# First mixer of a two-layer backbone: gate products on quarters of the array, ScalarE in order of issue, another order of the parts

## The chip, the cores and the metric

The kernel runs on one core of a Trainium2 chip. The metric is the device time of one execution in microseconds (us); lower is better. TensorE is called PE in the rows, VectorE DVE, ScalarE ACT, GpSimd POOL, and the queue of SyncE that issues nearly all DMAs is SP.

## What is computed

The reference is a backbone of two layers. Each layer has a SwiGLU sub-layer of half weight, a token mixer, and a second SwiGLU; each sub-layer is wrapped in RMSNorm with shift, scale and gate. There are 256 latent and 256 context tokens of width 1024. In the first layer the mixer runs on all 512 tokens. Its input projection has seven column groups: the RG-LRU's input and gate (512 columns each), three of 256 for a short gated convolution, and two of 256 for chunked spatial gating. The RG-LRU is what the change is about:

```python
def lru_coeffs(xc, w_r, b_r, w_i, b_i, lam):      # xc: tokens x 512, 8 heads of 64
    xh = xf.reshape(B, L, LRU_HEADS, HEAD_DIM)
    r = sigmoid(einsum('blhi,hij->blhj', xh, w_r) + b_r)
    i = sigmoid(einsum('blhi,hij->blhj', xh, w_i) + b_i)
    log_a = -LRU_C * r * softplus(-lam)
    a = exp(log_a)
    bx = sqrt(-expm1(2.0 * log_a)) * (i * xf)
    return a, bx                                  # for each of two directions
...
h = linear_scan(a, b, h0)                         # h[t] = a[t] h[t-1] + b[t]
o_lru = gelu(lru_gate) * (h_forward + h_backward)
```

The three branches are concatenated to 1024 channels and go through one output projection.

## The kernel before

**Layout.** Channels lie on the 128 partitions and the 512 tokens along the free axis. A matrix product of a weight tile is three products in a rounded type (`hi` x `hh`, `hi` x `hl`, `lo` x `hh`), so one unit of 128 output channels is 8 x 3 = 24 products of 512 columns. The raw weights come by DMA (`raw`, 512 KB), ScalarE casts them to `hi` in two halves, and VectorE subtracts for `lo` in two halves (`split`, L169). The gates' products are plain fp32.

**Parts of the mixer.** The mixer is written as parts with one letter each: `c`, `x`, `b` are the three units of the short convolution's channel groups 0 and 1 (`short_c`, `short_x`, `short_b`, L756 to L784), `g` the RG-LRU's gate branch (`gate`, L691), `v`, `u`, `m` the spatial gating (`chunk_v`, `chunk_u`, `chunk_mix`, L788 to L819). The RG-LRU's four channel groups (128 channels, two heads each) go through `C` (`lru_conv`, L709: one ScalarE and three VectorE instructions), `G` (`lru_gates`, L712: four products against `wbd`, four sigmoids, two multiplications), `D` (`lru_decay`, L726: for each direction an exponential, a tanh and three VectorE instructions) and `S` (`lru_scan`, L738: square roots, scans, the sum of the two directions, the gate, and `put`). `put` (L684) splits a finished group into `oh` (a cast on ScalarE) and `ol` (a subtraction on VectorE), the moving operands of the output projection.

**The gates' weights.** `wbd` of a channel group is one DMA of 256 KB: for each direction and gate a 128 x 128 matrix with the two heads' 64 x 64 blocks on its diagonal and zeros elsewhere. A group is four products of 128 x 128 by 512 columns (L717, L721), each with a PSUM bank of its own; `pbank` (L103) has six banks, and a product into a bank waits until the bank's last reader is done.

**What sets the order.** In the mixer PE runs in the order of the string `ORDER[0]` (`manual_schedule` with PE alone); the other engines' orders come from the scheduler. `unit` (L675) keeps three weight units in the queue. ScalarE holds one table of functions at a time; a sigmoid, an exponential or tanh, a square root and a GELU each need another, and a change is an `ACT_TABLE_LOAD`; copies, casts and scaled copies go with any.

**The output projection** (`out_phase`, L319) takes the channels in the order 4, 5, 6, 7, 0, 1, 2, 3, that is `b0`, `b1`, `m0`, `m1` and then the four RG-LRU groups. After it come the norms of the sub-layer and the second SwiGLU.

Of the kernel before, what the change touches and what calls it, by code (L numbers as in the profile page):

```python
# [8 lines left out]
F32 = mybir.dt.float32  # L9
# [36 lines left out]

LATE = ((0,), (1, 2, 3))
MANUAL = {mybir.EngineType.PE}

ORDER = ("c1 C0 g3 G0 C1 C2 C3 D0 c0 x1 G1 G3 D3 x0 S0 D1 v0 S3 G2 b0 g2 D2 u0 m0 S1 b1 u1 m1 S2",  # L50
         "c0 x0 C1 C0 C3 C2 g3 g2 G1 G0 D1 D0 c1 b0 u0 v0 S1 w0 G3 u1 x1 b1 m1 w1 S0 m0 G2 w2 p1 w3 w4 w5 p2 p5 w6 D2 S2 w7 p0 "
         "D3 S3 p7 p4 p3 p6")

TAIL = 4

# [26 lines left out]
def backbone(ctx: ExitStack, tc: tile.TileContext, xT, vecs, crow, w_mod, w_in, w_out, w_mi, w_mo, w_lru, w_cm, b_cm, lam, w_last, out):  # L82
# [20 lines left out]
    def pbank():  # L103
        return ps.tile([P, 512], F32, tag="mm", name=nm("mm"))
# [525 lines left out]
    def mixer(l, segs, nxt, plan, skew_out, order_of, next_unit=None):  # L630
# [77 lines left out]

        def lru_conv(c):  # L709
            xcs[c] = conv(c)  # L710

        def lru_gates(c):  # L712
            wbd = tp.tile([P, 4, P], F32, tag="wbd", name=nm("wbd"))
            nc.sync.dma_start(wbd, w_lru[l, c])
            for c, d, b in heads[2 * c:2 * c + 2]:
                pr = pbank()
                pe.matmul(pr, lhsT=wbd[:, 2 * d, :], rhs=xcs[c], start=True, stop=True)  # L717
                r = rs[c, d] = tt_()
                sc.activation(r, pr, AF.Sigmoid, bias=V("b_r", b))
                pi = pbank()  # L720
                pe.matmul(pi, lhsT=wbd[:, 2 * d + 1, :], rhs=xcs[c], start=True, stop=True)  # L721
                i = ix[c, d] = tt_()
                sc.activation(i, pi, AF.Sigmoid, bias=V("b_i", b))
                ve.tensor_tensor(i, i, xcs[c], op=OP.mult)

        def lru_decay(c):  # L726
            for c, d, b in heads[2 * c:2 * c + 2]:
# [114 lines left out]
        def out_part(k):  # L842
            for m in range(KT):
                out_mm(m, (k,))

        parts = dict(w=out_load, p=lambda m: out_mm(m, (4, 5, 6, 7)), g=gate, c=short_c, x=short_x, b=short_b, v=lambda _: chunk_v(), u=chunk_u, m=chunk_mix,
                     C=lru_conv, G=lru_gates, D=lru_decay, S=lru_scan)
        def issue():
            for part in order_of.split():
                parts[part[0]](int(part[1]))  # L850

        if len(segs) == 2:
            with tc.manual_schedule(engines=MANUAL):
# [5 lines left out]
            def load(m):
                hi, lo = unit()  # L860
                return (lambda k: hi[:, order[k], :]), (lambda k: lo[:, order[k], :])

            out_phase(range(KT), load, [oh[k] for k in order], [ol[k] for k in order], y, KT,
                      ranges(segs, skew_out), norms.on_y, 0, 1)
            return


# [383 lines left out]
```

## Time and profile before

| | us |
|---|---|
| median of 3 runs | 1642.15 (1640.8 to 1643.95) |
| the profiled execution: its own time | 1642.21 |
| the profiled execution: its span | 1640.4 |
| PE busy | 1612.5 |
| DVE busy | 1164.3 |
| ACT busy | 736.7 |
| POOL busy | 120.3 |

A span is the stretch from the first to the last instruction that the profile shows. Times such as 452.80 are us from its start. A row of a timeline gives the start, the duration, and the engine, line and operation, with the count of instructions that were merged; neighbouring instructions of one engine overlap by their tails, so what an instruction costs its engine is the step from its start to the next start. A matmul in fp32 shows as two records. The first mixer lies between about 441 and 572 us; its parts run on PE from 441.6 to 524.8, its output projection after that.

### The profile page before, as it was taken

How to read it: one execution, taken by the hardware profiler on the slowest of the kernel's cores; microseconds unless marked ns; L12 is line 12 of the kernel's file. 1: busy time of each engine (PE TensorE's matmuls, PEld its weight loads, DVE VectorE, ACT ScalarE, POOL GpSimd, SP SyncE). 2: the span in 40 equal slices, each digit the busy share in tenths (PEclk: the TensorE clock that was granted, in tenths of full speed). 3: DMA queues.
4: the chain of work that ended last, by engine and by line, in shares of the span. 5: the costliest groups of instructions: out<-in, count | busy, mean ns of one | idle time of the engine just before them, and what ended most of it. 6: DMA issues, size and time to landing. Idle time of an engine off the chain costs nothing.

```text
span 1640.4 us, 23432 instructions
## 1 busy us (share of the span) xinstructions
PE 1612.5 (98%) x8846; PEld 1371.6 (84%) x8846; DVE 1164.3 (71%) x2183; ACT 736.7 (45%) x1378; POOL 120.3 (7%) x166
## 2 busy tenths in 40 slices
PE   6999999999999999999999999999999999999998
PEld 3788888889977998888888998888888998789997
DVE  4899898548788787867763887767432788785554
ACT  5523322244697662332233462332232479864543
POOL 0000000005000500000000410000000410100000
PEclk9999999999999999999999999999999999999999
DMA  9577677431323225655552215655422316155552
GB/s 370 189 218 261 205 229 223 144 121 44 103 72 120 77 97 187 221 162 174 179 164 80 100 61 194 222 166 167 141 90 90 103 54 210 47 167 194 180 191 78
DMA packets 73906, 249.97 MB, mean 152 GB/s; under 512 B 8384, under 2 KB 10048, under 8 KB 73792
## 3 DMA queue, kind: packets, MB, share of 16 engines
q1 hardware_dynamic: 73216, 247.94, 45.9%
q8 instruction: 69, 1.13, 0.3%
q10 hardware_dynamic: 576, 0.52, 0.1%
q14 instruction: 45, 0.37, 0.1%
HBM read 247.39 MB, written 1.05 MB: 151 GB/s over the span
## 4 chain that ended last, share of the span: by engine, by line
PE 89%; DVE 6%; ACT 3%; DMA 1%; issue 1%; POOL 0%; SPq 0%; POOLq 0%; DVEq 0%; ACTq 0%
PE mm L113 87%; PE st L113 1%; DVE x L271 1%; DVE sq L394 1%; DVE t L703 0%; PE mod L113 0%; DVE z L270 0%; DVE tmp L262 0%; DMA x<-in_xT 0%; ACT hi L173 0%; DVE t L397 0%; POOL rs L241 0%; DVE t L332 0%; DMA raw<-in_w_mi 0%; ACT t L730 0%
## 5 line engine op out<-in xcount | busy, mean ns | idle before, releaser
L173 ACT CAST hi<-raw 128x512 fp32r<-128x512 f32 (+1 forms) x596 | 343.6, 610 | 672.7 <-PE mm L113 475.8
L113 PE MATMUL mm<-hh,hi 128*128 128x512 f32 (+1 forms) x1840 | 625.6, 348 | 0.5 <-ACT hh L1095 0.2
L113 PE MATMUL mm<-hl,hi 128*128 128x512 f32 (+1 forms) x1840 | 622.5, 346 | 1.8 <-DVE hl L256 1.0
L174 DVE TENSOR_TENSOR lo<-raw,hi 128x512 fp32r<-128x512 f32 (+1 forms) x596 | 387.5, 680 | 157.3 <-ACT hi L173 154.5
L113 PE MATMUL mm<-hh,lo 128*128 128x512 f32 (+1 forms) x1840 | 466.6, 346 | 0.0
L113 PEld LDWEIGHTS mm<-hh,hi 128*128 128x128 f32 x1840 | 345.5, 188 | 52.1 <-ACT hh L1095 2.8
L113 PEld LDWEIGHTS mm<-hl,hi 128*128 128x128 f32 x1840 | 345.9, 188 | 51.2 <-DVE hl L1101 1.6
L113 PEld LDWEIGHTS mm<-hh,lo 128*128 128x128 f32 x1840 | 325.1, 188 | 47.2
L196 DVE SCALAR_TENSOR_TENSOR junk<-raw,cb 128x1024 bf16<-128x1024 f32 x256 | 312.9, 1222 | 70.8 <-DMA raw<-in_w_mod 67.1
L113 PE MATMUL mm<-t,hi 128*128 128x512 f32 (+1 forms) x1056 | 240.6, 367 | 0.0
L113 PEld LDWEIGHTS mm<-t,hi 128*128 128x128 f32 x1056 | 182.8, 188 | 35.7 <-issue 0.2
L397 POOL TENSOR_TENSOR t<-t,sq 128x256 f32<-128x256 f32 x112 | 94.2, 856 | 712.2 <-ACT sq L391 702.3
L113 PE MATMUL mm<-t,lo 128*128 128x512 f32 (+1 forms) x528 | 131.5, 367 | 0.0
L113 PEld LDWEIGHTS mm<-t,lo 128*128 128x128 f32 x528 | 92.6, 188 | 17.7
L480 DVE TENSOR_TENSOR sg<-sg,mm 128x512 f32<-128x512 f32 (+1 forms) x72 | 45.9, 640 | 78.3 <-PE mm L113 78.3
L113 PE MATMUL mm<-t,hh 128*128 128x256 f32 x512 | 71.2, 281 | 0.0
L113 PEld LDWEIGHTS mm<-t,hh 128*128 128x128 f32 x512 | 65.7, 188 | 0.5
L173 ACT CAST t<-sg 128x512 fp32r<-128x512 f32 (+1 forms) x94 | 50.6, 541 | 32.0 <-DVE sg L480 29.0
L332 DVE TENSOR_TENSOR t<-t,mm 128x256 f32<-128x256 f32 (+1 forms) x66 | 35.4, 536 | 29.3 <-PE mm L113 29.1
L174 DVE TENSOR_TENSOR t<-sg,t 128x512 fp32r<-128x512 f32 (+1 forms) x94 | 55.3, 589 | 0.9 <-ACT t L173 0.9
L113 PE MATMUL mm<-hi,t 128*128 128x512 f32 x176 | 55.1, 394 | 0.0
L263 ACT ACTIVATE hh<-tmp,modv 128x256 fp32r<-128x256 f32 x72 | 42.4, 596 | 22.1 <-DVE tmp L262 21.9
(179 smaller groups left out, 1212.4 us busy)
## 6 DMA issues: line engine op xcount, KB each, us to landing
raw<-in_w_in SPq DMA_DIRECT2D x176, 512.0 KB, 3.6
raw<-in_w_mod SPq DMA_DIRECT2D x128, 512.0 KB, 4.3
raw<-in_w_out SPq DMA_DIRECT2D x48, 512.0 KB, 3.3
raw<-in_w_mi SPq DMA_DIRECT2D x36, 512.0 KB, 4.1
raw<-in_w_last SPq DMA_DIRECT2D x22, 512.0 KB, 3.3
raw<-in_w_out SPq DMA_DIRECT2D x24, 384.0 KB, 3.7
t<-in_w_mod SPq DMA_DIRECT2D x32, 256.0 KB, 5.8
raw<-in_w_mo SPq DMA_DIRECT2D x8, 512.0 KB, 3.7
```

The costliest lines, as they stand in the source:

```text
L113: te.matmul(dst, lhsT=lhsT, rhs=rhs, start=start, stop=stop)
L173: sc.copy(hi, src)
L174: ve.tensor_tensor(lo, src, hi.bitcast(F32), op=OP.subtract)
L196: ve.scalar_tensor_tensor(junk, raw.rearrange("p k c -> p (k c)"), 1.0, cb[:, s], op0=OP.mult, op1=OP.mult, accum_out=modv[l][:, v, m, s:s ...
L263: sc.activation(hh[:, m, a:b], tmp, AF.Identity, scale=A, bias=B)
L271: ve.scalar_tensor_tensor(x[:, m, a:b], z, mcol(l, 3 * i + 2, m, s), x[:, m, a:b], op0=OP.mult, op1=OP.add)
L332: ve.tensor_tensor(y[m][:, a:b], y[m][:, a:b], p[:, :b - a], op=OP.add)
L394: ve.scalar_tensor_tensor(q[2], y, G, x[:, m, a:b], op0=OP.mult, op1=OP.mult)
L397: (gp if JACC[c] == "g" else ve).tensor_tensor(acc[c], acc[c], q[c], op=OP.add)
L480: ve.tensor_tensor(sg[:, :b - a], sg[:, :b - a], pu[:, :b - a], op=OP.mult)
```

## The change

Four things change, all in the first mixer (`l` = 0, both segments); layer 1's order string is only rewritten for the new letters.

1. **Gates on quarters** (`QUARTERS`). The 64 x 64 blocks alone are multiplied. For each direction and gate there are two products, each on 64 rows of the array and 64 of its columns: gate `r` reads partitions 0 to 63, gate `i` partitions 64 to 127, head 0 writes partitions 0 to 63 of the bank and head 1 partitions 64 to 127. So that both gates find both heads in their rows, a copy of the convolution's result with its halves exchanged (`swap`, two tiles) is made by two DMAs from POOL's queue in `C`. The weights come in four DMAs of 32 KB instead of one of 256 KB. There are 32 products of 64 x 64 instead of 16 of 128 x 128, and 8 POOL DMAs and 12 SP DMAs more.
2. **ScalarE in order of issue.** In the first mixer's parts ScalarE, too, runs in the written order.
3. **Another `ORDER[0]`.** The short convolution's and the gates' parts are placed anew; square roots are a part of their own (`R`) ahead of the scans (`S`), `put` is a part of its own (`H`), and `l4`, `l5` fill the queue of weight units to four or five.
4. **Output projection.** The first five output tiles are begun (`EARLY`) with channels 4 to 7, twelve products each, and ended later with channels 0 to 3.

```diff
-ORDER = ("c1 C0 g3 G0 C1 C2 C3 D0 c0 x1 G1 G3 D3 x0 S0 D1 v0 S3 G2 b0 g2 D2 u0 m0 S1 b1 u1 m1 S2",
+IN_ORDER = {mybir.EngineType.PE, mybir.EngineType.Activation}
+ORDER = ("c1 C0 C1 g3 C2 C3 c0 G0 G1 l4 D0 D1 x1 l5 R0 R1 S0 S1 G3 x0 l5 G2 D3 D2 H0 b0 l5 H1 v0 g2 l4 u0 R3 R2 m0 S3 b1 "
+         "u1 m1 l4 S2 H3 H2",
...
         def lru_conv(c):
             xcs[c] = conv(c)
+            if l in QUARTERS:
+                lru_swap(c)
+        def lru_swap(c):
+            t = turned_xc[c] = tp.tile([P, T], F32, tag="swap", name=nm("swap"), bufs=2)
+            for a, b in ((0, P // 2), (P // 2, 0)):
+                gp.dma_start(t[a:a + P // 2], xcs[c][b:b + P // 2])
+        def gate_products(c):
...
+                        nc.sync.dma_start(wbd[64 * g:64 * g + 64, :, h], src[a:a + 64, :, g, a:a + 64])
...
+            def products(d):
+                ps2 = pbank(), pbank()
+                for g, p in enumerate(ps2):
...
+                    for h in range(2):
+                        src = (xcs if g == h else turned_xc)[c]
+                        rows, cols = slice(64 * g, 64 * g + 64), slice(64 * h, 64 * h + 64)
+                        pe.matmul(p[cols], lhsT=wbd[rows, d, h], rhs=src[rows], start=True, stop=True)
+                return ps2
...
         def lru_gates(c):
-            wbd = tp.tile([P, 4, P], F32, tag="wbd", name=nm("wbd"))
-            nc.sync.dma_start(wbd, w_lru[l, c])
+            products = gate_products(c)
             for c, d, b in heads[2 * c:2 * c + 2]:
-                pr = pbank()
-                pe.matmul(pr, lhsT=wbd[:, 2 * d, :], rhs=xcs[c], start=True, stop=True)
+                pr, pi = products(d)
...
+        def lru_root(c):
+            for d in range(2):
+                sc.activation(rs[c, d], rs[c, d], AF.Sqrt, scale=-1.0)
         def lru_scan(c):
...
-                sc.activation(h, h, AF.Sqrt, scale=-1.0)
...
-            put(c, h)
+        def lru_put(c):
+            put(c, rs[c, 1])
...
-            with tc.manual_schedule(engines=MANUAL):
+            with tc.manual_schedule(engines=IN_ORDER if l in QUARTERS else MANUAL):
                 issue()
...
+            for item in todo[:EARLY]:
+                begun.append(begin(item))
+            for i, (m, a, b) in enumerate(todo):
+                p = begun[i] if i < EARLY else begin(todo[i])
+                half(p, m, a, b, 1)
+                sc.copy(y[m][:, a:b], p[:, :b - a])
+                norms.on_y(m, a, b)
```

How the change moves instructions shows on two engines. In the names the first number is the buffer's. On PE, group 2's gates of the kernel before stand between `v0` (the last products of `mm_667`) and `b0` (`mm_682`):

```order
L113 MATMUL mm_667_4272<-hi_649_4112,hl_80 128x256
L113 MATMUL mm_671_4313<-t_615_3960,wbd_670_4311 128x512
L113 MATMUL mm_673_4317<-t_615_3960,wbd_670_4311 128x512
L113 MATMUL mm_675_4322<-t_615_3960,wbd_670_4311 128x512
L113 MATMUL mm_677_4326<-t_615_3960,wbd_670_4311 128x512
L113 MATMUL mm_682_4339<-hh_79,hi_657_4178 128x512
```

After the change the same gates are eight quarter products, between `x0` (`mm_661`) and `b0` (`mm_680`), with no `v0` ahead of them; `mm_666`, `mm_667`, `mm_670` and `mm_671` are their four banks:

```order
L119 MATMUL mm_661_4185<-hh_79,lo_614_3965 128x512
L119 MATMUL mm_666_4231<-t_608_3946,wbd_665_4226 64x512
L119 MATMUL mm_666_4231<-swap_609_3951,wbd_665_4226 64x512
L119 MATMUL mm_667_4232<-swap_609_3951,wbd_665_4226 64x512
L119 MATMUL mm_667_4232<-t_608_3946,wbd_665_4226 64x512
L119 MATMUL mm_670_4242<-t_608_3946,wbd_665_4226 64x512
L119 MATMUL mm_670_4242<-swap_609_3951,wbd_665_4226 64x512
L119 MATMUL mm_671_4243<-swap_609_3951,wbd_665_4226 64x512
L119 MATMUL mm_671_4243<-t_608_3946,wbd_665_4226 64x512
L119 MATMUL mm_680_4281<-hh_79,hi_636_4053 128x512
```

Group 2's gates now stand ahead of `v0`, right behind `x0`; each bank takes two products, and the last bank used before them is `x0`'s instead of one of `v0`'s. On ScalarE, the sigmoids of groups 1 and 3 in the kernel before (L719 and L723 are the sigmoids, L741 the square root, L730 the exponential):

```order
L719 ACT_TABLE_LOAD
L719 ACTIVATE t_630_4062<-mm_629_4060,vec_76 128x512
L723 ACTIVATE t_632_4066<-mm_631_4064,vec_76 128x512
L719 ACTIVATE t_634_4071<-mm_633_4069,vec_76 128x512
L723 ACTIVATE t_636_4075<-mm_635_4073,vec_76 128x512
L719 ACTIVATE t_639_4082<-mm_638_4080,vec_76 128x512
L723 ACTIVATE t_641_4086<-mm_640_4084,vec_76 128x512
L741 ACT_TABLE_LOAD
L741 ACTIVATE t_611_3948<-t_611_3948 128x512
L719 ACT_TABLE_LOAD
L719 ACTIVATE t_643_4091<-mm_642_4089,vec_76 128x512
L723 ACTIVATE t_645_4095<-mm_644_4093,vec_76 128x512
```

After the change group 3's sigmoids (`mm_653` to `mm_658`) come behind the square roots of groups 0 and 1, and those behind the casts of two weight units and the last tanh (L771 is the tanh, L780 the square root, L761 and L763 the sigmoids):

```order
L771 ACTIVATE t_633_4046<-t_633_4046,s4_100 128x512
L179 CAST hi_647_4126<-raw_646_4124 128x512 x2
L179 CAST hi_650_4134<-raw_649_4132 128x512 x2
L780 ACT_TABLE_LOAD
L780 ACTIVATE t_620_4008<-t_620_4008 128x512
L780 ACTIVATE t_624_4019<-t_624_4019 128x512
L780 ACTIVATE t_629_4035<-t_629_4035 128x512
L780 ACTIVATE t_633_4046<-t_633_4046 128x512
L761 ACT_TABLE_LOAD
L761 ACTIVATE t_655_4169<-mm_653_4163,vec_76 128x512
L763 ACTIVATE t_656_4171<-mm_654_4164,vec_76 128x512
L761 ACTIVATE t_659_4180<-mm_657_4174,vec_76 128x512
```

ScalarE now does one function for several groups before it changes the table, and the sigmoids that free group 3's banks stand further back in its queue.

## Rows read from the trace of the kernel before

**Rows 1.** The page: busy time of PE, and the chain by engine.

```profile
PE 1612.5 (98%) x8846; PEld 1371.6 (84%) x8846; DVE 1164.3 (71%) x2183; ACT 736.7 (45%) x1378; POOL 120.3 (7%) x166
...
PE 89%; DVE 6%; ACT 3%; DMA 1%; issue 1%; POOL 0%; SPq 0%; POOLq 0%; DVEq 0%; ACTq 0%
```

**Rows 2.** Busy time by window: start:end, length, PE PEld DVE ACT POOL, clock.

```profile
480.00:490.00 10.00, 10.00 (x88) 10.00 (x87) 10.00 (x21) 9.92 (x16) 0.00 (x0) 1.00 0.08 29
```

**Rows 3.** All waits of PE between 400 and 600: total, times, longest.

```profile
PE st L113 <- POOL t L397: 0.2, 1, 0.2
```

**Rows 4.** Timeline of PE: a unit of 24 products, and three gate blocks.

```profile
447.20 0.40 PE L113 MATMUL mm<-hh,hi 128*128 128x512 f32 x1
...
452.80 3.59 PE L113 MATMUL mm<-t,wbd 128*128 128x512 f32 x8
...
456.46 0.39 PE L113 MATMUL mm<-hl,hi 128*128 128x512 f32 x1
...
467.43 7.03 PE L113 MATMUL mm<-t,wbd 128*128 128x512 f32 x16
...
474.52 0.39 PE L113 MATMUL mm<-hl,hi 128*128 128x512 f32 x1
```

**Rows 5.** Timeline of PE: fp32 products on 32 columns, and on 64 (`chunk_mix`).

```profile
34.54 1.93 PE L113 MATMUL mod<-t,cs 128*32 128x512 f32 x16
...
36.73 0.40 PE L113 MATMUL mm<-hl,hi 128*128 128x512 f32 x1
...
511.41 1.09 PE L113 MATMUL mm<-wcm,t 128*64 128x128 f32 x16
```

**Rows 6.** Timeline of ACT: casts, table load, sigmoids, exponentials, square roots, GELUs.

```profile
437.03 3.25 ACT L173 CAST hi<-raw 128x512 fp32r<-128x512 f32 x6
...
454.41 1.28 ACT L719 ACT_TABLE_LOAD   x1
455.70 0.69 ACT L719 ACTIVATE t<-mm,vec 128x512 f32<-128x512 f32 x1
...
458.00 2.24 ACT L701 ACTIVATE t<-t,vec 128x512 f32<-128x512 f32 x3
...
461.55 1.34 ACT L730 ACTIVATE t<-t,s 128x512 f32<-128x512 f32 x2
...
484.77 1.16 ACT L741 ACTIVATE t<-t 128x512 f32<-128x512 f32 x2
...
491.12 1.21 ACT L798 ACTIVATE t<-mm 128x256 f32<-128x256 f32 x4
```

**Rows 7.** Timeline of DVE: the decay's instructions, a convolution step, the scans.

```profile
482.01 1.29 DVE L732 SCALAR_TENSOR_TENSOR t<-t,t 128x512 f32<-128x512 f32 x2
...
484.42 0.76 DVE L735 TENSOR_SCALAR t<-t 128x512 f32<-128x512 f32 x2
485.09 0.48 DVE L778 SCALAR_TENSOR_TENSOR t<-zc,vec,t 128x256 f32<-128x256 f32 x1
...
488.48 1.22 DVE L744 TENSOR_TENSOR_SCAN t<-t,t 128x512 f32<-128x512 f32 x1
489.61 0.67 DVE L747 TENSOR_TENSOR_SCAN t<-t,t 128x256 f32<-128x256 f32 x1
```

**Rows 8.** DMA issues of the gates' weights between 425 and 530: size, us to landing.

```profile
wbd<-in_w_lru SPq DMA_DIRECT2D x4, 256.0 KB, 2.9
```

**Rows 9.** Timeline of DVE: one instruction beside busy POOL, and after it.

```profile
540.24 0.96 DVE L394 SCALAR_TENSOR_TENSOR sq<-t,modv,x 128x256 f32<-128x256 f32 x1
...
550.95 0.48 DVE L394 SCALAR_TENSOR_TENSOR sq<-t,modv,x 128x256 f32<-128x256 f32 x1 [0.53 <-ACT t L330]
```

**Rows 10.** Windows in the second mixer's end, columns as in rows 2.

```profile
1434.00:1438.00 4.00, 3.02 (x26) 2.94 (x24) 3.14 (x6) 1.60 (x4) 0.00 (x0) 0.93 0.37 110
1438.00:1442.00 4.00, 4.00 (x20) 3.87 (x19) 2.43 (x11) 1.62 (x3) 1.90 (x2) 0.50 0.43 155
1442.00:1446.00 4.00, 2.69 (x12) 1.99 (x11) 3.32 (x10) 2.29 (x4) 0.39 (x1) 0.72 0.38 133
```

More of the change, by code (lines that the diff above doesn't have):

```diff
@@ L37 @@
 NSQ = 3
+QUARTERS = (0,)
+EARLY = 5
 JACC = 'gvg'
@@ L710, in lru_conv @@
             xcs[c] = conv(c)
+            if l in QUARTERS:
+                lru_swap(c)
+        turned_xc = {}
+        def lru_swap(c):
[3 more added lines that the diff above has]
+        def gate_products(c):
+            if l in QUARTERS:
+                wbd = tp.tile([P, 2, 2, P // 2], F32, tag="wbd", name=nm("wbd"))
+                for g in range(2):
+                    for h in range(2):
+                        a = 64 * h
+                        src = w_lru[l, c].rearrange("p (d g) o -> p d g o", g=2)
+                        nc.sync.dma_start(wbd[64 * g:64 * g + 64, :, h], src[a:a + 64, :, g, a:a + 64])
+            else:
+                wbd = tp.tile([P, 4, P], F32, tag="swap", name=nm("wbd"))
+                nc.sync.dma_start(wbd, w_lru[l, c])
+            def products(d):
+                ps2 = pbank(), pbank()
+                for g, p in enumerate(ps2):
+                    if l not in QUARTERS:
+                        pe.matmul(p, lhsT=wbd[:, 2 * d + g, :], rhs=xcs[c], start=True, stop=True)
+                        continue
+                    for h in range(2):
+                        src = (xcs if g == h else turned_xc)[c]
+                        rows, cols = slice(64 * g, 64 * g + 64), slice(64 * h, 64 * h + 64)
+                        pe.matmul(p[cols], lhsT=wbd[rows, d, h], rhs=src[rows], start=True, stop=True)
+                return ps2
+            return products
         def lru_gates(c):
-            wbd = tp.tile([P, 4, P], F32, tag="wbd", name=nm("wbd"))
-            nc.sync.dma_start(wbd, w_lru[l, c])
+            products = gate_products(c)
             for c, d, b in heads[2 * c:2 * c + 2]:
-                pr = pbank()
-                pe.matmul(pr, lhsT=wbd[:, 2 * d, :], rhs=xcs[c], start=True, stop=True)
+                pr, pi = products(d)
                 r = rs[c, d] = tt_()
                 sc.activation(r, pr, AF.Sigmoid, bias=V("b_r", b))
-                pi = pbank()
-                pe.matmul(pi, lhsT=wbd[:, 2 * d + 1, :], rhs=xcs[c], start=True, stop=True)
                 i = ix[c, d] = tt_()
@@ L736, in lru_decay @@
                 es[c, d] = e
+        def lru_root(c):
+            for d in range(2):
+                sc.activation(rs[c, d], rs[c, d], AF.Sqrt, scale=-1.0)
         def lru_scan(c):
-            for c, d, _ in heads[2 * c:2 * c + 2]:
+            for d in range(2):
                 e, h, b = es[c, d], rs[c, d], ix[c, d]
-                sc.activation(h, h, AF.Sqrt, scale=-1.0)
                 ve.tensor_tensor(b, b, h, op=OP.mult)
@@ L846, in mixer @@
         parts = dict(w=out_load, p=lambda m: out_mm(m, (4, 5, 6, 7)), g=gate, c=short_c, x=short_x, b=short_b, v=lambda _: chunk_v(), u=chunk_u, m=chunk_mix,
-                     C=lru_conv, G=lru_gates, D=lru_decay, S=lru_scan)
+                     C=lru_conv, G=lru_gates, D=lru_decay, R=lru_root, S=lru_scan, H=lru_put, l=fill)
         def issue():
@@ L857, in mixer, with half, begin @@
             y = norms.y = [tt_() for _ in range(KT)]
[L859 to L864, printed above, removed]
+            todo, begun, ws = ranges(segs, skew_out), [], {}
+            def half(p, m, a, b, i):
+                hi, lo = ws[m]
+                ops = [(hi, x_, k) for k in order[4 * i:4 * i + 4] for x_ in (oh, ol)]
+                ops += [(lo, oh, k) for k in order[4 * i:4 * i + 4]]
+                for j, (w, x_, k) in enumerate(ops):
+                    pe.matmul(p[:, :b - a], lhsT=w[:, k, :], rhs=x_[k][:, a:b], start=i == j == 0, stop=i == 1 and j == len(ops) - 1)
+            def begin(item):
+                if item[0] not in ws:
+                    ws[item[0]] = unit()
+                p = pbank()
+                half(p, *item, 0)
+                return p
+            for item in todo[:EARLY]:
[5 more added lines that the diff above has]
+                norms.on_y(m, a, b)
             return
@@ L873, in mixer @@
         need(nxt[0], 3 * nxt[1] + 1)
-        with tc.manual_schedule(engines=MANUAL):
+        with tc.manual_schedule(engines=IN_ORDER if l in QUARTERS else MANUAL):
             issue()
@@ L877, in mixer @@
                 out_part(k)
-        with tc.manual_schedule(engines=MANUAL2):
+        with tc.manual_schedule(engines=MANUAL2 | IN_ORDER if l in QUARTERS else MANUAL2):
             pieces = unit_pieces(next_unit)
```

4 lines of the change are left out of this document (2 added, 2 removed).

## The prediction

> **What bounds the kernel now.** I read the page first, then the windows over the first mixer, then PE's waits, then the timelines. PE is busy in 1612.5 of 1640.4 us and is 89% of the chain that ended last [rows 1]. In the mixer it is busy without a break: the window at 480 shows 10.00 of 10 us at clock 1.00, and between 400 and 600 PE's waits come to 0.2 us [rows 2, 3]. So the mixer now costs what PE's columns cost, and whatever ScalarE or VectorE saves there is worth nothing by itself. But the same window has VectorE at 10.00 and ScalarE at 9.92 [rows 2]: PE is only just ahead of two full engines. The question is whether they still keep pace when PE does its gates earlier and in less time.
>
> **The change part by part.** The sum is made against the profiled execution, 1642.21 us, which is the median within 0.1 us.
>
> Gate products, removed: a unit of 24 products takes 5.60 us (447.20 to 452.80), a product 0.233. The first gate block begins at 452.80; the next unit's second product begins at 456.46, its first 0.23 earlier, so four gate products take 3.43 us, 0.857 each, and the double block 6.86 (467.43 to 474.52, less 0.23) [rows 4]. The third block equals the first: 16 products, 13.7 us.
>
> Gate products, added: 32 quarter products of as many columns. If four run side by side, they cost 8 x 0.857 = 6.9 us, a gain of **6.9**; if two, 13.7 and no gain; if none, 27.4 and a loss of 13.7. No row shows products on half the rows. The nearest are eight fp32 products of 32 columns of the array: from 34.54 to the next product (36.73 less 0.23) they take 1.96 us, which is 0.98 for four against 4 x 0.857 alone, so four ran together, with about 0.1 us at each change of shape [rows 5]. I take four together, and 8 changes at 0.1: +0.8. The Trainium skill, "TensorE: Matmul & The Clock Gate", Part 3 (Packing small matmuls), says that weights are loaded beside running products only where the row group differs; the two heads of a gate here share one. By it only pairs would run together (a rival below); the rows just read, four column tiles in one row group, speak against it.
>
> ScalarE's table: the new order changes tables 9 times less at 1.29 us (454.41 to 455.70) [rows 6]. PE does not wait for ScalarE there now, so that is worth nothing by itself. What counts is where each result stands in ScalarE's queue, which is now fixed.
>
> First new wait, at G2. In the new order `c1 g3 c0` are the units at 441.6, 447.2 and 452.8, so `c0` ends at 458.4. ScalarE's copy of `c0` stands ahead of the sigmoids. By steps [rows 6]: cast or copy 3.25/6 = 0.54, table 1.29, sigmoid (458.00 - 455.70)/4 = 0.575, exponential or tanh 0.62 (1.34 for two, less a tail of 0.1), square root 0.58 (1.16 for two). So: copy to 459.1; table 460.4; eight sigmoids of G0 and G1 465.0; four casts (`l4`) 467.1; table 468.4; eight exponentials and tanh 473.4, and 0.4 for tanh that now follow their own exponential, 473.8; four casts (`l5`) 476.0; table 477.2; four square roots 479.5; table 480.8; three of G3's sigmoids 482.5. PE meanwhile: G0 and G1 458.4 to 462.1, and 0.25 because G1's last banks wait for G0's sigmoids; `x1` to 468.0; G3 to 469.8; `x0` to 475.4; G2 would end at 477.2. But there are six banks: four hold G3's results, one `x0`'s, and G2 has four to write. Its second, third and fourth wait for G3's first three sigmoids, so G2's last pair of products starts at 482.6 and ends at 483.1. New wait: **+5.9** us. `b0` and all behind it on PE stand in the queue.
>
> Second new wait, at `m1`. VectorE works off the decays without a break from the first tanh (about 469.8). I count 64 instructions up to `b0`'s product: 35 at 0.60, 8 at 0.33, 15 short ones at 0.39, 4 half scans at 0.6, 2 scans at 1.13 [rows 7] = 34 us, so it ends about 504. ScalarE comes to the cast of `b0` about 493 and, being in order, stands there until VectorE has made it, 504.7. Behind it: four casts, a table, `v0`'s GELUs (1.21 for four [rows 6]), `g2`'s 0.6, and the cast of `u1`'s weights, to 510.5; VectorE needs that cast, idles from 507, and then has 27 instructions (19 at 0.60, 4 at 0.6, 2 at 1.13, and 1.6 of waits) before `m1`'s last product: 17.7 us, to 528.3, product 528.9, ScalarE's cast 529.5. PE hides most: from 483.2 `b0` 5.6, `v0` 11.2, `g2` 5.6, `u0` 5.6, `m0` 0.9 [rows 5], `b1` 5.6, `u1` 5.6, `m1` 0.9 come to 524.2, and twelve products of the two first output tiles with three of the four channels to 527.0. New wait: about +2.7, and some 0.6 for the third tile's parked weights, whose casts ScalarE has behind it: **+3.3**. Later channels (0 to 3) are covered by the other begun tiles.
>
> At nothing: the swaps (4 pairs of DMAs). C0's and C1's convolutions end near 452 and 452.5 on VectorE, G0 and G1 need them at 458.4 and 460.3; the nearest landing is 2.9 us [rows 8]. C2's and C3's wait for G0's and G1's products, and their users G3 and G2 are ahead of ScalarE anyway. The 12 more SP issues, the earlier weights and layer 1's `wbd` in the swaps' tiles cost SP time while SP has units in hand; if that cover went, one landing, 2.9. Begun output tiles: same products.
>
> Sum: -6.9 + 0.8 + 0.25 + 5.9 + 3.3 = **+3.35**: 1645.6 us. Both waits are set by ScalarE and VectorE, so what PE saves or loses ahead of them moves the sum little.
>
> **The rivals.**
> A, no new wait: ScalarE or VectorE get through 6 to 7 us faster than their rows say, and the quarters' gain shows. For it: PE had no wait at all before with more table loads [rows 3]. Against: 23 us of the chain to G3's sigmoids are counted in rows. -6.9 + 1.0 = 1636.3.
> B, the forecast: 1645.6; own range 1643 to 1648.
> C, pairs only, or the change doesn't do what it says: no gain on PE, but the wait at G2 shrinks from 5.9 to 1.5 since ScalarE sets its end, so only +1.8 more: 1647.4. If none runs together, PE is the bound again: 1642.2 + 13.7 + 0.8 and the second wait, about 1659.
> D, slower by late swaps: POOL issues four DMAs between 452 and 458 while VectorE runs the convolutions. VectorE's L394 takes 0.96 beside busy POOL and 0.48 after it [rows 9]: the two hinder each other. It decides from 4 p + 2.9 = 8.3, p = 1.3 us for one issue on POOL; at p = 2, G1 starts 2.6 late, the whole ScalarE queue moves with it: 1648.2. The Trainium skill, "SBUF — State Buffer" (A bandwidth-pool intuition that's wrong), gives such a DMA about 0.62 us alone and 3.1 beside a copy on VectorE; by 3.1, worked out as an estimate, it would be 7 late and 1652. No row shows a DMA from POOL.
> E, slower by the clock: at 1434, after PE was busy in only 3.02 of 4 us, its granted clock fell from full speed (2.4 GHz) to 0.50 (1.2 GHz); it was down for some 6 us [rows 10]. A drop behind the wait at G2 is mostly hidden by the second wait, which VectorE sets; behind the second it is not: half of 6 us, 1648.6.
>
> **How the numbers follow.** B 0.60, A 0.10, C 0.12 (0.05 of it with none together), D 0.08, E 0.10. What a measurement of this kernel tells from no change is 0.2%, 3.3 us: below 1638.9 or above 1645.4. Faster: A and a little of B, 0.12. Slower: more than half of B (0.32), all of C, D and E but a little: 0.58. Same: 0.30. The range leaves out most of A and the loss of the unpaired quarters: 1640 to 1651.
>
> **What would show it.** Steps right: gate blocks of 1.7 to 1.9 us each; PE idle some 6 us before `b0`, put down to ScalarE's sigmoid; an idle stretch of 2 to 4 us about 527 to 531, ended by a cast on ScalarE; ScalarE idle some 10 us before about 505. Wrong: gate blocks of 3.4 (C); PE waiting for a DMA before G0 or G1 (D); clock under 1.00 between 480 and 540 (E); no waits at all (A). The forecast is wrong if ScalarE reaches G3's sigmoids before 477, or if VectorE's 64 instructions take under 30 us.

## The result: 0.6 % slower, and the profile after

The changed kernel takes 1652.45 us (median of 4 runs, 1651.09 to 1655.18) against 1643.05 for the kernel before on the same chip (4 runs, 1640.8 to 1646.17). The ratio is 1.0058, with a 95 % interval of 1.0041 to 1.0074: some 9.4 us slower. The direction was forecast; the size was not, and the time lies above the range.

The profiled execution after has a span of 1650.7 us against 1640.4. To see where the 10.3 us arise I take one mark on either side of the first mixer: two SiLU instructions of ScalarE, one in the first SwiGLU and one in the second. Timelines of ScalarE (start, duration, engine, line, operation), first of the kernel before, then of the changed one:

```profile
341.71 0.59 ACT L479 ACTIVATE sg<-mm 128x512 f32<-128x512 f32 x1
...
608.01 0.38 ACT L479 ACTIVATE sg<-mm 128x256 f32<-128x256 f32 x1
```

```profile
343.69 0.59 ACT L485 ACTIVATE sg<-mm 128x512 f32<-128x512 f32 x1
...
619.40 0.38 ACT L485 ACTIVATE sg<-mm 128x256 f32<-128x256 f32 x1
```

From mark to mark it is 266.30 us before and 275.71 after: the mixer costs **+9.41**. The first mark itself is 1.98 late. That is no work of the change: in the experiments below, whose code ahead of this mark is the same, the mark comes between 1.33 us earlier and 1.74 later than in the kernel before. So the stretch from mark to mark is what I compare from here on; whole times are compared by their ratio. Each stretch comes from one profiled execution, and executions of one kernel differ by several us (1640.8 to 1646.17 for the kernel before), so differences of a us or two between stretches decide nothing by themselves.

The page hardly shows it: PE's busy time and the chain by engine, to be read beside [rows 1].

```profile
PE 1617.7 (98%) x8878; PEld 1372.8 (83%) x8878; DVE 1166.2 (71%) x2183; ACT 725.0 (44%) x1369; POOL 124.8 (8%) x174
...
PE 86%; DVE 7%; ACT 3%; DMA 1%; POOL 1%; issue 1%; SPq 0%; POOLq 0%; DVEq 0%; ACTq 0%
```

PE is busy for 5.2 us more, though the gates' columns were cut by half on paper; VectorE and POOL take a per cent more of the chain.

All waits of PE between 400 and 620 after (total, times, longest), where the kernel before had 0.2 us between 400 and 600 [rows 3]:

```profile
PE mm L119 <- ACT t L761: 2.7, 1, 2.7
PE mm L119 <- issue: 1.6, 1, 1.6
PE mm L119 <- ACT t L179: 1.3, 1, 1.3
PE st L119 <- POOL t L403: 1.0, 2, 0.8
PE mm L119 <- ACT hh L179: 0.3, 1, 0.3
```

Both forecast waits are there, the one for G3's sigmoid (L761) and the one for `m1`'s cast (L179). But they come to less than forecast: 4.3 instead of 5.9 at G2 (2.7 and 1.6), and 1.6 instead of 3.3 at `m1` (1.3 and 0.3). The 1.0 for POOL lies behind the mixer, about 567, and was not forecast. Yet the loss is nearly three times the forecast. The rest does not stand under waits. It stands in the windows (start:end, length, busy time of PE PEld DVE ACT POOL, granted clock, DMA share, GB/s), to be held against 10.00 and 1.00 before [rows 2]:

```profile
470.00:480.00 10.00, 8.44 (x44) 5.28 (x44) 8.66 (x19) 9.83 (x15) 0.00 (x0) 1.00 0.40 131
480.00:490.00 10.00, 7.26 (x22) 3.28 (x22) 10.00 (x17) 9.95 (x16) 0.00 (x0) 0.62 0.41 132
490.00:500.00 10.00, 10.00 (x58) 8.79 (x58) 10.00 (x21) 6.09 (x10) 0.00 (x0) 0.86 0.10 22
...
510.00:520.00 10.00, 10.00 (x55) 7.87 (x54) 3.25 (x6) 5.95 (x12) 0.00 (x0) 1.00 0.50 159
...
530.00:540.00 10.00, 8.41 (x42) 5.99 (x41) 10.00 (x18) 7.34 (x13) 0.00 (x0) 0.86 0.49 159
540.00:550.00 10.00, 10.00 (x60) 8.82 (x60) 6.89 (x12) 5.37 (x11) 0.00 (x0) 0.97 0.91 320
```

The clock falls twice. At its two levels, 1.00 (2.4 GHz) and 0.50 (1.2 GHz), means of 0.62 and 0.86 over 10 us each are 2 x (0.38 + 0.14) x 10 = 10.4 us at the lower level; they begin at 482.5, still within the wait at G2. In the same way 0.86 and 0.97 are 3.4 us behind the wait at `m1`. PE counts as busy at either level, so the busy column does not tell. The second thing to see is VectorE, 3.25 of 10 us at 510: it was full there in the forecast.

PE's timeline shows the blocks and the place where the clock falls:

```profile
460.46 0.64 PE L119 MATMUL mm<-t,wbd 64*64 64x512 f32 x1
...
464.79 0.50 PE L119 MATMUL mm<-hh,hi 128*128 128x512 f32 x1
...
470.59 0.64 PE L119 MATMUL mm<-t,wbd 64*64 64x512 f32 x1
...
472.46 0.50 PE L119 MATMUL mm<-hh,hi 128*128 128x512 f32 x1
...
479.89 0.61 PE L119 MATMUL mm<-t,wbd 64*64 64x512 f32 x1 [1.56 <-issue]
...
483.79 1.11 PE L119 MATMUL mm<-swap,wbd 64*64 64x512 f32 x1 [2.74 <-ACT t L761]
...
487.40 0.79 PE L119 MATMUL mm<-hh,hi 128*128 128x512 f32 x1
```

G3's eight quarter products take 1.87 us (470.59 to 472.46) where four full ones took 3.43 [rows 4]; G0 and G1 together take 4.33. (The 3.43 went by the second product of the next unit. By that reading G3 takes 1.98.) In G2 a record is 0.61 us long at 479.89 and 1.11 at 483.79: from there PE runs at half speed, and `b0` begins at 487.40.

ScalarE from G3's sigmoids on, and VectorE (L761 a sigmoid, L179 a cast, L701 `g2`'s GELU, L850 `u0`'s, L780 the square roots of R3 and R2; for VectorE L818 is the short convolution's last reading of `x1`'s bank, L861 `m0`'s sum):

```profile
481.76 1.28 ACT L761 ACT_TABLE_LOAD   x1
483.05 0.69 ACT L761 ACTIVATE t<-mm,vec 128x512 f32<-128x512 f32 x1
...
506.71 0.62 ACT L179 CAST t<-t 128x512 fp32r<-128x512 f32 x1 [10.48 <-DVE t L828]
...
512.50 0.60 ACT L701 ACTIVATE t<-mm 128x512 f32<-128x512 f32 x1 [1.08 <-PE mm L119]
...
518.11 0.60 ACT L850 ACTIVATE t<-mm 128x512 f32<-128x512 f32 x1 [2.94 <-PE mm L119]
...
520.01 2.20 ACT L780 ACTIVATE t<-t 128x512 f32<-128x512 f32 x4
...
535.11 0.62 ACT L179 CAST t<-t 128x512 fp32r<-128x512 f32 x1 [0.23 <-DVE t L863]
```

```profile
479.38 0.41 DVE L818 TENSOR_TENSOR zl<-t,mm 128x256 f32<-128x256 f32 x1
...
513.64 2.50 DVE L180 TENSOR_TENSOR lo<-raw,hi 128x512 fp32r<-128x512 f32 x4 [3.78 <-ACT hi L179]
519.14 0.69 DVE L861 TENSOR_TENSOR t<-mm,bcm 128x512 f32<-128x512 f32 x1 [3.00 <-PE mm L119]
```

Here the loss is passed on. ScalarE waits for PE at `g2` and at `u0` (1.08 and 2.94); the square roots stand behind `u0`'s GELU in its fixed order. VectorE stands still for 3.78 us, until the cast that ScalarE makes behind `g2`'s GELU, and for 3.00, until PE's `m0`; the scans of groups 3 and 2, which need the square roots, follow at 520.68, and from there it works with almost no break to `m1`'s sum. (The first square root and `m0`'s sum both end about 520.6, so the trace does not tell which of the two held the scans; both waited for PE.) So `m1`'s cast at 535.11 is late because PE was late, not because VectorE had too much to do.

### The profile page after: what moved, and what is told of

It reads as the page before. It is cut to its first block, busy times and chain, and to the rows that moved or that the text cites. A ratio compares the mean times of both kernels' runs of the same rounds, so it can differ in the third digit from the quotient of the medians.

```text
span 1650.7 us, 23532 instructions
## 1 busy us (share of the span) xinstructions
PE 1617.7 (98%) x8878; PEld 1372.8 (83%) x8878; DVE 1166.2 (71%) x2183; ACT 725.0 (44%) x1369; POOL 124.8 (8%) x174
## 4 chain that ended last, share of the span: by engine, by line
PE 86%; DVE 7%; ACT 3%; DMA 1%; POOL 1%; issue 1%; SPq 0%; POOLq 0%; DVEq 0%; ACTq 0%
PE mm L119 84%; PE st L119 1%; DVE x L277 1%; POOL t L403 1%; PE mod L119 1%; ACT hi L179 1%; DVE sq L400 1%; DVE lo L180 1%; DMA wo<-in_w_mo 0%; DVE t L709 0%; DVE z L276 0%; DVE tmp L268 0%; DMA x<-in_xT 0%; DVE t L403 0%; ACT t L770 0%
## 5 line engine op out<-in xcount | busy, mean ns | idle before, releaser
L179 ACT CAST hi<-raw 128x512 fp32r<-128x512 f32 (+1 forms) x596 | 343.0, 610 | 675.3 <-PE mm L119 475.4
L179 ACT CAST t<-sg 128x512 fp32r<-128x512 f32 (+1 forms) x94 | 50.6, 541 | 27.5 <-DVE sg L486 24.4
```

The lines of the kernel that those rows point to most:

```text
L179: sc.copy(hi, src)
```

## Theories

- **T**: the order on ScalarE makes a wait at G2; behind it PE's clock falls; and the time lost there is not hidden, since in this order VectorE's scans wait for PE's products, by way of ScalarE.
- **V**, as in the forecast: VectorE's work sets `m1`'s put whatever PE does, so a delay of PE behind G2 is hidden.
- **Q**: the quarters themselves cost the time, by swaps from POOL or by the small DMAs.

The runs in one table. "Mixer" is the stretch from mark to mark less 266.30; "low" is the time at the lower clock between 440 and 580, from the windows as above. The kernel before was run again beside each: its medians are 1644.43 us beside the four kernels that follow the change in the table, 1644.48 beside the next four, and 1645.12 beside the three called spread.

| kernel | ratio to before, 95 % | mixer, us | PE's largest waits, us | low, us |
|---|---|---|---|---|
| the change | 1.0058 (1.0041 to 1.0074) | +9.4 | 2.7, 1.6, 1.3 | 10.4 + 3.4 |
| ScalarE free | 0.9989 (0.9974 to 1.0003) | +0.1 | 1.7, 0.7, 0.5 | 0 |
| quarters alone | 1.0008 (0.9995 to 1.0021) | +3.4 | 2.0, 0.8 | 7 |
| order alone | 1.0045 (1.0026 to 1.0065) | +7.2 | 1.8, 1.3, 1.1 | 3.4 |
| 22 fillers at G2 | 1.0026 (1.0013 to 1.0039) | +4.05 | 1.3, 0.8, 0.3 | 0 |
| 40 fillers at G2 | 1.0054 (1.0033 to 1.0074) | +11.7 | 2.4, 0.8, 0.3 | 3.4 + 3.4 |
| no begun tiles | 1.0040 (1.0027 to 1.0053) | +5.8 | 2.7, 1.6, 1.3 | 6.8 |
| no wait at G2 | 1.0016 (1.0005 to 1.0027) | +5.2 | 4.2, 0.5 | 6.8 |
| G3 first | 1.0013 (1.0003 to 1.0023) | +3.0 | 2.0, 1.7, 0.9 | 3.4 |
| spread | 0.9996 (0.9984 to 1.0008) | +1.7 | 2.5, 0.5 | 6.8 |
| spread, full products | 1.0026 (1.0014 to 1.0039) | +4.5 | 1.2, 0.6 | 3.4 |
| spread, ScalarE free | 0.9969 (0.9958 to 0.9981) | -2.5 | 1.2, 0.7 | 0 |

## Experiments on the cause

**ScalarE free.** The change with ScalarE's order left to the scheduler:

```diff
-IN_ORDER = {mybir.EngineType.PE, mybir.EngineType.Activation}
+IN_ORDER = {mybir.EngineType.PE}
```

> The changed kernel with one part undone: in the first mixer ScalarE's order comes from the scheduler again; PE keeps the new order, the quarters stay. Theory T: the cost comes from the wait at G2 that ScalarE's written order makes, and from the drop of PE's clock behind it. Then PE's wait ahead of G2 is under 1.5 us, the granted clock between 480 and 500 is 1.00, and the time is about 1645 us (7 less than the changed kernel; the quarters' own gain partly shows). Rival Q, the quarters and their DMAs cost the time: the waits at G2 go, but the time stays above 1650. Rival V, VectorE's chain to m1's put alone sets the end: also above 1650, with PE's wait near 530 longer by what it gains at G2.

Measured: 1645.35 us, ratio 0.9989, mixer +0.1. PE's waits (400 to 620):

```profile
PE mm L119 <- ACT t L179: 2.2, 2, 1.7
PE mm L119 <- ACT t L761: 0.7, 1, 0.7
...
```

The wait for G3's sigmoid is gone but for 0.7 us, the clock stays at 1.00, and with quarters, swaps, small DMAs and PE's order all in place the loss is gone. Q falls for the change: the cost is ScalarE's order.

**Quarters alone, order alone.** The kernel before with the quarters and swaps only; and the change with `QUARTERS = ()` (and ScalarE in order where `l == 0`).

> The kernel before with one part of the change alone: gate products on quarters with their swaps and small DMAs; the old order of the parts, ScalarE by the scheduler, the old output projection. Theory T: the quarters themselves save about 6 us of PE, but the old order leaves each swap no time, so PE waits for POOL's DMAs at G0, G1, G3, G2 by 1 to 3 us each; together about 1 us slower than before, 1643 to 1645, and no clock below 1.00 in 440 to 560 unless one wait is above 3 us. Rival Q: 1649 or more. Had the quarters been free of waits: 1637.

> The changed kernel without the quarters: full 128 x 128 gate products, no swaps, one DMA for each group's weights; the new order, ScalarE in order and the begun output tiles stay. Theory T: PE reaches G2 about 5 us later (three gate blocks at 3.4 instead of 1.8), the wait there is about 2 us instead of 4.3, the clock falls for a shorter time or not at all, and the time is 1647 to 1650. If the clock falls for the same 10 us, 1651 to 1653. Rival Q: as fast as before, 1643, since the quarters that cost the time are gone. Rival V: 1648, with a wait near 530 of 2 to 3 us and a clock of 1.00 all along.

Measured: 1646.83 us (ratio 1.0008) and 1652.83 (1.0045). The quarters alone cost the mixer 3.4 us in the profiled execution, where in the old order PE waits for the swaps; over all runs the difference from the kernel before is not clear of zero. The clock falls after a wait of 2.0 us; the expectation had excluded that below 3 us, a bound that no run shows. PE's waits, then the windows at 470 and 480, of the quarters alone:

```profile
PE mm L114 <- DMA swap<-t: 2.8, 2, 2.0
...
```

```profile
470.00:480.00 10.00, 7.97 (x37) 2.96 (x37) 10.00 (x21) 8.66 (x13) 1.03 (x2) 0.82 0.22 60
480.00:490.00 10.00, 10.00 (x53) 8.66 (x52) 8.94 (x19) 7.29 (x12) 0.00 (x0) 0.83 0.29 110
```

The order alone costs 7.2 us, and its time is above the 1647 to 1650 that T gave. Its wait at G2 is 1.8 us as T said, with the clock at 1.00 behind it; the waits together (1.8, 1.3, 0.3, and 1.3 for POOL) are 4.7, a fall of the clock from 562.1 on, behind POOL's wait, costs half of 3.4, and the rest of some 0.8 is not placed. The order is thus bad without the quarters too. The two parts do not add up to 9.4 (10.6), and need not, since a wait takes in what was saved ahead of it.

**The clock apart from the wait.** The change with 22 products ahead of G2 into a bank that nobody reads, so that PE works where it would wait:

```diff
...
+                for j in range(n // 2):
+                    te.matmul(st, lhsT=hh[:, 0, 0:P], rhs=hh[:, 0], start=True, stop=True)
```

> The changed kernel with 22 more products of 128 x 128 by 512 columns ahead of G2, into a bank that nobody reads: they fill 5.1 us in which PE otherwise waits, and nothing else is changed (the results stay the same). It tells the cost of the clock from the cost of the wait. Theory T: the granted clock stays 1.00 from 480 to 500, b0 and all behind it end about 4.3 us earlier, ScalarE's square roots and m1's put follow, and the time falls by 3 to 5.5 us, to 1647 to 1649.5, though PE has 5 us more work. Rival V, VectorE's chain sets m1's put whatever PE does: the clock stays up, but the wait near 531 grows by what is gained, and the time is within 0.7 us of the changed kernel (1652.45). Rival: the filler delays G2 itself, 1653 to 1654.

Measured: 1650.4 us, ratio 1.0026; the mixer is +4.05 instead of +9.41, though PE has 5.2 us more work. The time itself is 0.9 above the expected range, but the kernel before was slower too on this occasion (1644.43). By the ratios, whose intervals do not overlap, the gain over the change is 0.32 %, 5.3 us. Timeline of PE, one window, timeline of ScalarE:

```profile
476.11 5.17 PE L761 MATMUL fill<-hh 128*128 128x512 f32 x22
481.21 0.64 PE L120 MATMUL mm<-t,wbd 64*64 64x512 f32 x1
...
483.90 0.50 PE L120 MATMUL mm<-hh,hi 128*128 128x512 f32 x1
```

```profile
480.00:490.00 10.00, 10.00 (x50) 6.54 (x49) 10.00 (x16) 9.93 (x15) 0.00 (x0) 1.00 0.45 133
```

```profile
504.65 0.62 ACT L180 CAST t<-t 128x512 fp32r<-128x512 f32 x1 [10.45 <-DVE t L837]
...
512.20 0.60 ACT L859 ACTIVATE t<-mm 128x512 f32<-128x512 f32 x1 [0.29 <-PE mm L120]
...
514.11 2.20 ACT L789 ACTIVATE t<-t 128x512 f32<-128x512 f32 x4
...
529.21 0.62 ACT L180 CAST t<-t 128x512 fp32r<-128x512 f32 x1 [0.22 <-DVE t L872]
```

The clock stays at 1.00. This run's first mark is at 341.62, that of the change at 343.69, so 2.07 is taken off each difference: `u0`'s GELU comes 5.91 - 2.07 = 3.84 us earlier than in the change, the square roots 3.83, `m1`'s cast 3.83. What the clock lost at G2 reaches `m1` whole; VectorE's two standstills shrink from 3.78 and 3.00 to 2.58 and 0.35. The other 1.5 of the 5.36 us is the second fall, which this run does not have either (3.4 us at half speed, 1.7). That part is no work of the fillers as far as the runs show: the wait at `m1` is as long as in the change, and with no begun tiles (below), too, the same wait has no fall behind it. V is wrong, T holds.

**A delay without the clock.** To see the passing-on alone, there are 40 fillers instead of 22: PE is late, but its clock is up.

> As the kernel with 22 filling products ahead of G2, but with 40: PE now reaches G2 some 3.8 us after the wait has ended, with its clock up all along. It tells whether a delay of PE behind G2 is hidden by the wait at m1, as the prediction's rival E held. Theory T (ScalarE, in order, holds R3's and R2's square roots back behind the GELUs of g2 and u0, so PE's delay passes on to VectorE's scans and to m1's put): 2.5 to 4 us slower than with 22, in the stretch from 441 to 608 too, some +6.5 to +8 against the kernel before. Rival, hidden by VectorE's chain: at most 1 us slower than with 22, and the wait near 531 shrinks by the rest.

Measured: 1653.13 us, ratio 1.0054 against 1.0026 with 22, and in the profile the mixer is +11.7, 7.6 more than with 22. The profiled execution, 1658.98, is the slowest of only four (from 1649.64), and the two intervals overlap, so the whole time does not settle it; the places of the instructions do. Timelines of PE and ScalarE (first mark at 342.88, so 1.26 is taken off):

```profile
488.43 0.50 PE L120 MATMUL mm<-hh,hi 128*128 128x512 f32 x1
```

```profile
516.73 0.60 ACT L859 ACTIVATE t<-mm 128x512 f32<-128x512 f32 x1 [2.94 <-PE mm L120]
...
518.64 2.20 ACT L789 ACTIVATE t<-t 128x512 f32<-128x512 f32 x4
```

`b0` starts 488.43 - 483.90 - 1.26 = 3.27 us later, and the square roots come 518.64 - 514.11 - 1.26 = 3.27 later: nothing is hidden. The wait at `m1` grows to 2.4, and there and at 568 the clock falls in this profiled run, each time for 3.4 us, which costs half of that. The expectation's 2.5 to 4 left these falls out.

**No begun tiles.** `EARLY = 0`, the rest as in the change.

> The changed kernel with the output projection undone in part: no output tile is begun ahead (each takes its channels 4 to 7 and then 0 to 3 at once). Theory T: the loss lies ahead of the output projection, and the first output tile waits for m1's put at its channel 7 in either form, so the time stays 1651 to 1654 with the same wait at G2 and the same fall of the clock. Rival: the begun tiles hold banks or move ScalarE's work, and undoing them gives back 2 us or more (below 1650.5). Other rival: they cover the late channels 0 to 3, and without them it is 2 us or more slower.

Measured: 1651.79 us, ratio 1.0040, mixer +5.8 in the profile. The waits at G2 and at `m1` are the same to the tenth. The stretch is 3.6 us shorter: the clock is low for 6.8 us instead of 10.4 at G2, where nothing ahead differs, and not at all at `m1`, and POOL's wait is 0.2 instead of 1.0. The intervals of the two kernels overlap: what the begun tiles cost or give is not settled here.

## Orders without the wait

**G3 first** moves G3 ahead of D0, D1, R0, R1, S0 and S1. PE's own order stays, but D0 and D1 also come behind `x1` and `l5`, whose casts ScalarE now does earlier:

```diff
-... G0 G1 l4 D0 D1 x1 l5 R0 R1 S0 S1 G3 x0 ...
+... G0 G1 l4 x1 l5 G3 D0 D1 R0 R1 S0 S1 x0 ...
```

> The changed kernel with one move in the order: G3 stands ahead of D0, D1, R0, R1, S0 and S1, so that its sigmoids come right behind those of G0 and G1 in ScalarE's queue; all else as in the changed kernel. Theory T: no wait at G2 and no fall of the clock at 482; small waits of some 2 us stay near 483 (v0's banks wait for G2's sigmoids), 502 and 525, so the mixer is 1.5 to 4 us longer than in the kernel before instead of 9.4: 1645 to 1648, if none of these lets the clock fall; 1.7 us more for each that does. Rival V, the wait at m1 sets the end whatever happens at G2: 1651 to 1653.

Measured: 1647.17 us, ratio 1.0013, mixer +3.0 (one fall of 3.4 us near 528), as T expected. This one move in ScalarE's queue is worth 6.4 of the 9.4 us.

**No wait at G2** goes further: G3 first, scans and puts at the end, `g2` as the last unit, and for each direction `1 - e` on ScalarE.

```diff
+ORDER = ("c1 C0 C1 g3 C2 C3 c0 G0 G1 l4 x1 l5 G3 D0 D1 x0 l5 G2 b0 l5 R0 R1 v0 D3 D2 R3 R2 l4 u0 m0 u1 m1 b1 l3 g2 l4 S0 S1 S3 S2 H0 H1 H3 H2",
...
+            order = [4, 6, 7, 5, 0, 1, 2, 3]
```

> The changed kernel with another order of the parts, made so that nothing waits at G2: G3's gates ahead of the decays of groups 0 and 1, scans and puts of the RG-LRU at the end, g2 as the last unit; the output projection takes its channels as 4, 6, 7, 5, 0 to 3; and one VectorE instruction for each direction and group (1 - e) goes to ScalarE. ScalarE stays in order, the quarters stay. Theory T: with no wait at G2 the clock stays at 1.00 from 440 to 520, the quarters' 6 us show in part (VectorE's work is the next bound, with a wait of 2 to 3.5 us near 518), and the mixer is 1 to 3.5 us shorter than in the kernel before: 1641 to 1644. Rival, the quarters and their DMAs cost time wherever they stand, or ScalarE's order costs by itself: slower than the kernel before by 3 us or more. If the clock falls behind the wait near 518: 1.7 us more.

Measured: 1647.76 us, ratio 1.0016: a miss. PE waits 0.7 us in the mixer's parts, as wanted, and then once for POOL. Timelines of POOL and PE:

```profile
547.96 3.76 POOL L402 TENSOR_TENSOR t<-t,sq 128x256 f32<-128x256 f32 x4 [0.60 <-DVE sq L399]
552.33 6.04 POOL L402 TENSOR_TENSOR t<-t,sq 128x256 f32<-128x256 f32 x7 [0.60 <-DVE sq L399]
```

```profile
557.55 2.72 PE L118 MATMUL st<-ones,t 128*128 128x2 f32 x12 [4.20 <-POOL t L402]
```

A begun tile ends every 12 products, 2.8 us, and gives POOL four additions for the norm, 3.76 us: POOL falls behind, PE waits 4.2 us, and the clock falls for 6.8 us. So the begun tiles can have a cost through POOL; that it shows only where PE is not late is argued, not tested.

**Spread**: the same with `EARLY = 4` and half of one accumulation on VectorE; then without the quarters; then with ScalarE left to the scheduler.

```diff
-                    (gp if JACC[c] == "g" else ve).tensor_tensor(acc[c], acc[c], q[c], op=OP.add)
+                    (ve if JACC[c] == "v" or (self.l, self.i) == (0, 1) and c == 2 and n % 2 else gp).tensor_tensor(acc[c], acc[c], q[c], op=OP.add)
```

> The order without a wait at G2 again, with two changes for what its first run showed (POOL's accumulation for the norm behind the mixer ended 4.2 us late, and the clock fell behind that wait): four begun output tiles instead of five, and in that norm half of one accumulation's pieces go from POOL to VectorE. If POOL's wait and the clock behind it were what ate the gain: no wait of PE above 1.5 us between 540 and 580, clock 1.00 from 440 to 580, the mixer 2 to 4 us shorter than in the kernel before, 1640.5 to 1642.5. Rival: VectorE, with more to do, ends the norm late by itself, and nothing is won against the order's first run, 1646 to 1648. If the clock falls behind a wait of some 2.5 us near 518: 1.7 us more.

> As the kernel with four begun tiles and the spread accumulation, but without the quarters: full 128 x 128 gate products, no swaps, one DMA for each group's weights. It prices the quarters in an order in which nothing waits at G2. The gate blocks cost 6.1 us more on PE, and the wait near 518 shrinks by some 2 us: 3 to 5 us slower than with the quarters, and the mixer 0 to 2 us longer than in the kernel before. Rival, VectorE alone sets the mixer's length whatever PE does: the same time as with the quarters, within 1 us.

> As the kernel with four begun tiles and the spread accumulation, but with ScalarE's order from the scheduler. Theory T says that ScalarE's written order costs only where it puts something late that PE waits for; in this order it does not, so the two are within 1.5 us of each other, and this one is 2 to 4.5 us faster than the kernel before, 1640 to 1642.5, with waits of at most 1 us and no fall of the clock between 440 and 580. Rival, ScalarE in order costs by itself: this one is 3 us or more faster than the one in order.

Measured: 1644.0 (ratio 0.9996), 1649.45 (1.0026) and 1639.66 (0.9969), beside 1645.12 for the kernel before. The first is a miss: POOL's wait is down to 0.2, but a wait of 2.5 near 531 comes, the clock falls, and the mixer is +1.7 instead of 2 to 4 us shorter. Since begun tiles and accumulation were changed together, which of them helped POOL is not settled. The second is slower than the first as expected, but its mixer is +4.5 instead of 0 to 2. The quarters are worth 2.8 us of mixer here and 0.3 % by the ratios, with intervals that do not overlap, so in this order they do save time. The third beats both kernels. That ScalarE in order costs nothing here was wrong: the two differ by 4.2 us in the mixer. Timelines of PE and ScalarE in order, then ScalarE by the scheduler (`hh<-raw` is the cast of a parked output weight):

```profile
531.66 2.38 PE L118 MATMUL mm<-t,hi 128*128 128x512 f32 x4 [2.50 <-ACT t L178]
```

```profile
530.47 0.62 ACT L178 CAST hh<-raw 128x512 fp32r<-128x512 f32 x1 [2.52 <-DMA raw<-in_w_mo]
531.00 0.61 ACT L178 CAST t<-t 128x512 fp32r<-128x512 f32 x1
```

```profile
522.90 1.14 ACT L178 CAST t<-t 128x512 fp32r<-128x512 f32 x2
526.45 0.62 ACT L178 CAST hh<-raw 128x512 fp32r<-128x512 f32 x1 [2.41 <-DMA raw<-in_w_mo]
```

In order, the cast of a put (531.00), for which PE waits, stands behind a cast whose weights have not landed; the clock is then low for 6.8 us. The scheduler put two of these casts ahead of the same late DMA, and PE did not wait there.

## Why the prediction was right or wrong

- **Gate products** (-6.9 + 0.8): right. Four run together; G3 takes 1.87 against 1.8, G0 and G1 4.33 against 3.95. Running in pairs, G3 would have taken 3.4, so rival C fell. The Trainium skill, "TensorE: Matmul & The Clock Gate", Part 3 (Packing small matmuls), says that a weight load overlaps running products only where the row group differs; "pairs only" was the prediction's own conclusion from it, and the trace speaks against that conclusion.
- **The wait at G2**: right in place and releaser. ScalarE's table load ahead of G3's sigmoids ends at 483.05, less 1.98 for the shift 481.07, against 480.8. Of the forecast 5.9 us 4.3 show as waits; the products behind them then ran at half speed (483.79 to 487.40). Part of the wait (1.56, put down to issue) comes before G2's first product, for which I had assumed a free bank. By the order of the six banks it is `x1`'s, and the trace agrees: VectorE's last reading of `x1` (L818) ends at 479.79, and the product starts at 479.89.
- **The second wait**: right in place and in its end where the clock stays up, wrong in size. With 22 fillers the cast of `b0` comes at 504.65 (forecast 504.7) and `m1`'s at 529.21 (forecast 529.5). But PE comes to `m1` at 528.6 instead of 527.0, and the wait there is 1.6 against 3.3. That this kernel's mixer, +4.05, is near the forecast +3.35 is so far partly luck: PE's later arrival makes up for the shorter wait, and POOL's 1.0 us was not in the sum.
- **The step that failed is rival E's**, "a drop behind the wait at G2 is mostly hidden by the second wait, which VectorE sets". In the sum it was priced at nothing, and it was given, with the second fall, a chance of 0.10. The clock is worth 5.36 us (9.41 - 4.05): 3.84 at G2, passed on whole, and 1.5 at `m1`, a fall that other runs with the same wait lack. The first half of VectorE's chain is as forecast: in the change, too, `b0`'s cast comes at 506.71 - 1.98 = 504.73. Behind it the working had counted ScalarE's queue by its own durations, and not by what its entries wait for: R3's and R2's square roots stand behind the GELUs of `g2` and `u0`, which wait for PE, and VectorE itself stands until `m0`'s product. So VectorE's chain to `m1` hangs on PE, and no slack was there to hide anything (with 22 fillers `u0`'s GELU already waits 0.29 us for PE). The chance was too low as well: [rows 10] showed a fall after less idle time than the forecast itself expected at G2, and its windows give 6.8 us at the lower level, not 6.
- **Rival D** fell for the change: POOL issues four swap DMAs in 2.24 us, 0.56 each, and PE waits for none. In the old order (quarters alone) PE does wait, 2.8 us; there the first swap is issued 2.6 us ahead of G0's products (453.87 to 456.45), in the change 6.0 (454.46 to 460.46). [rows 9] are also weaker than they were read: at 549.07 the same instruction took 0.49 us with POOL still busy. The Trainium skill, "SBUF — State Buffer" (A bandwidth-pool intuition that's wrong), gives 3.1 us for a DMA from GpSimd's queue beside a copy on VectorE; the forecast's estimate took that as the time of one issue. Here VectorE ran no copy but its convolution steps (L709): an issue took 0.56 us, and the data landed 3.2 us after it. A timeline of POOL after, and its DMA issues between 440 and 480:

```profile
454.46 2.24 POOL L726 DMA_DIRECT2D swap<-t  x4 [33.99 <-DVE t L709]
```

```profile
swap<-t POOLq DMA_DIRECT2D x8, 128.0 KB, 3.2
```

- **Rival A** and the begun tiles "at nothing": the waits came, so A fell. The tiles need not be at nothing, since they press on POOL (no wait at G2). In the change itself they show as a wait for POOL of 1.0 us against 0.2 without them, which stays inside the runs' spread.

What stays open: why the clock stays low for 10.4 us in the change and for 6.8 with no begun tiles, though all ahead of it is the same; and which waits let it fall. Waits of 1.7 (G3 first, at 485), 1.75 (ScalarE free) and 1.8 us (order alone, at G2) left it at 1.00, and it fell behind waits of 2.0 (quarters alone, G3 first). But it also fell behind the wait of 1.3 and 0.3 at `m1` in the change, which left it up with 22 fillers and with no begun tiles, and behind POOL's waits of 1.1 (order alone) and 0.8 (40 fillers), while the same 0.8 left it up with 22. So the length of a single wait does not tell, and the price of a wait cannot be computed here beforehand.

## What to carry to other kernels

When an engine is put in a written order, follow its queue instruction by instruction up to the end of the forecast stretch, and mark each entry that waits for the engine you think is ahead: that is where a delay comes back. Before a wait of a few microseconds on a full TensorE is priced at its own length, add the time at half clock behind it, and count it as hidden only if the engine that should hide it does not itself wait for TensorE. A few products into an unread bank told the clock from the wait here.

## What the runs showed of the hardware

- Eight fp32 products on quarters of the array, two row halves by two column halves, take 1.87 us (1.98 read like the full ones) where four full ones take 3.43: four run side by side, and those on the same rows too.
- Filling a wait with useless work made the kernel faster: 5.2 us more of products, 5.36 us less mixer, of which 3.84 because the granted clock stayed at 1.00 at G2; 0.32 % over all runs.
- POOL's 128 x 256 additions took 0.94 us each (3.76 for four) with VectorE busy for 3.3 of 4 us, so four to a tile keep pace with tiles of 5.6 us and not with tiles of 2.8.
- The fall of the clock did not go by the length of one wait: a wait of 1.8 us left it at 1.00, and in other runs it fell behind 1.1 and 0.8.
